# A two-layer decoder step on one core: scores of two heads side by side, running sums as split products, samples' values by transposes

## The chip, the cores and the metric

The kernel runs on one core of a Trainium2 chip. The metric is the device time of one execution in microseconds, as the median of several executions. TensorE multiplies (PE in the profile; its weight loads are PEld), VectorE (DVE), ScalarE (ACT) and GpSimd (POOL) do the rest, and SyncE (SP) issues most transfers.

## What is computed

Two layers of a decoder for a prompt of 256 tokens and eight samples of one token each (position 256), which share all weights: 264 columns in all. Layer 0 mixes by softmax attention in blocks (with 256 keys there is one block, so it is plain causal attention) beside a gated MLP over positions; layer 1 by stick-breaking attention beside causal pooling. After each comes a feed-forward block with a short convolution. Cut to the two attentions:

```
# layer 0, per head
s = q @ k.T * scale;  s = where(causal, s, -inf);  out = softmax(s) @ v
# layer 1, per head
z = q @ k.T * scale
log_keep = where(before, log_sigmoid(-z), 0)
later    = reverse_cumsum(log_keep) - log_keep
w        = where(before, exp(log_sigmoid(z) + later), 0);  out = w @ v
```

A sample's query attends to 256 cached keys, which lie in two pages of 128 per sample, and in layer 0 to its own key as well.

## The kernel before, in words

Activations lie with the features on the 128 partitions and the 264 columns along the free dimension. Every projection is a sum over blocks of 128 x 128 weights. Each weight and each activation is split into a rounded fp32r part and the fp32r rest (h and l), and each block takes three products of 264 columns, h·h, h·l and l·h (lines 334 to 336, the tile mm). The weights come by DMA in chunks; ScalarE makes wh (L311) and VectorE wl (L312) for eight blocks at a time, up to three such tiles ahead, in four buffers.

The order of the projections is fixed by `run`: it goes through the blocks of a phase, and after every eighth block (with fractions allowed) it calls the hooks entered for that point. A hook's number is the count of groups of eight blocks done, less one. The phases are in0, out0, ff0, dn0, in1, out1, ff1, dn1. The hooks hold everything else: page loads, scores, softmax, products with V, the mixers. They only give the order in which the program is written; a planner then places the instructions of each engine by a simulation of its own, as operands and buffers become free, and may move a hook's work behind later projection blocks. Instructions wrapped in `keep_in_program_order` keep their order among each other. Each engine then runs its list strictly in the planned order. PSUM has eight banks: four for projections (psm), four for all else (psa, made by `at`).

What the change touches:

- `s_qk` (lines 650 to 667), layer 0, one head: scores of query block 0 with key block 0 (L654, 128 columns) and of query block 1 with both key blocks (L655, 256 columns), fp32 with 64 rows of contraction, then two bf16 products of the identity with the causal mask (L656, L657), all in one bank; then two maxima on VectorE, two exponentials with sums on ScalarE, and the scaling, into a tile p. `s_tr` transposes p on TensorE (L675), `s_av` multiplies with V (L499, L500).
- `z_qk` (864 to 874), layer 1, one head: scores with keys on the partitions (L868, 256 columns; L869, 128), the masks (L870, L871), and `softplus` (858 to 862: three ScalarE steps, one VectorE step) into L.
- `z_cum` (876 to 882): the reverse running sum along the keys, as a product of a triangle of -1 with L (L880, 384 columns, fp32) and of all -1 with the second key block (L881, 128 columns, fp32), added onto the scores in their bank, and one exponential (L882) into w. Hooks: z_qk of head h at 5 + h, z_cum one hook later.
- The samples: `sample_score` (L456) in column groups of 32, `sample_av` (L470) the products with V, of which VectorE keeps each head's own 64 columns by a mask (L472), and `sample_out` (L483), which gathers them by products with a selection matrix of 8 columns. `sm_out` (721) and `zs_out` (913) put the result into the columns 256 to 263 of catA. In layer 0 sample scores come at hooks 6.5 and 9, their softmax at 10.25; in layer 1 `zs_soft` and `zs_cum` come at 11 and 12, the products with V at 13 and 14.

catA and catB are the operands of the output projection, which reads catB first.

Of the kernel before, what the change touches and what calls it, by code (L numbers as in the profile page):

```python
# [9 lines left out]
F32 = mybir.dt.float32  # L10
F32R = mybir.dt.float32r
# [7 lines left out]
P = 128  # L19
# [3 lines left out]
NS = 8  # L23
# [20 lines left out]
YD = ((0, 1), (1, 2), (2, 4), (4, 6), (6, 8))  # L44
YQ = 1

SC0 = 6.5
SC1 = 9
SGL = 6
GG = 16  # L50
GM = 12
# [1 line left out]
GN = 16.1  # L53
SQK = 5
STR = 7
SSO = 10.25
STP = 12
GT = 17
GA = 17.5
# [11 lines left out]
ZQ1 = 1  # L71
ZC = 1
PM = 13
ZSS = 11
ZSC = 12
ZSA = 13
ZSO = 14.75
NA = 4
# [95 lines left out]
def _consts():  # L174
    f = np.float32
    parts = []

    def add(name, a):
        full = np.zeros((P, a.shape[1]), f)
        full[: a.shape[0]] = a  # L180
        _CST[name] = (sum(x.shape[1] for x in parts), a.shape[1])
        parts.append(full)

    half = 8
    inv = (f(500000.0) ** (-(np.arange(half, dtype=f) * f(2.0) / f(16)))).astype(f)
# [15 lines left out]
    add("bm", (r[:, None] % 32 == h8[None, :]).astype(f))  # L201
    add("selS", np.concatenate([(r[:, None] // 32 + 4 * g == h8[None, :]) for g in range(2)], 1).astype(f))
# [24 lines left out]
def tile_decoder_step(ctx: ExitStack, tc: tile.TileContext, a):  # L227
# [4 lines left out]
    rawp = ctx.enter_context(tc.tile_pool(name="rawp", bufs=3))  # L232
    wsp = ctx.enter_context(tc.tile_pool(name="wsp", bufs=4))
    up = ctx.enter_context(tc.tile_pool(name="up", bufs=24))
    pp = ctx.enter_context(tc.tile_pool(name="pp", bufs=6))
    sm = ctx.enter_context(tc.tile_pool(name="sm", bufs=3))
    psm = ctx.enter_context(tc.tile_pool(name="psm", bufs=MMB, space=PSUM))
    psa = ctx.enter_context(tc.tile_pool(name="psa", bufs=8 - MMB, space=PSUM))
# [226 lines left out]
    def sample_av(msk, pz, vtiles, gr, name):  # L465
        pv = at(f"pv_{name}{gr}")
        for pg in range(NPG):
            for j in range(4):
                sq = 4 * gr + j
                pe.matmul(pv[32 * j:32 * j + 32, :], pz[:, pg, sq, :], vtiles[sq][:, pg, :],  # L470
                          start=pg == 0, stop=pg == NPG - 1)
        v.tensor_tensor(msk[:, gr], pv.rearrange("p (h d) -> p h d", d=HD),  # L472
                        cst("bm").unsqueeze(2).to_broadcast([P, NH, HD]), ALU.mult)

    def sample_av_of(st, pz, vtiles, gr, name):
        return lambda: sample_av(st["msk"], pz, vtiles, gr, name)

    def sample_out(msk, name):

        po = at(f"po_{name}")  # L480
        for t in range(4):
            for gr in range(2):
                pe.matmul(po[:, t * NS:(t + 1) * NS], msk[:, gr, 2 * t:2 * t + 2, :].rearrange("p h d -> p (h d)"),  # L483
                          cst("selS")[:, gr * NS:(gr + 1) * NS],
                          start=t == 0 and gr == 0, stop=t == 3 and gr == 1, skip_group_check=True)
# [130 lines left out]
    maskb0 = con.tile([P, P], BF16, name="maskb0")  # L616
    maskb1 = con.tile([P, P], BF16, name="maskb1")
    identb = con.tile([P, P], BF16, name="identb")

    def masks():  # L620
        tc.keep_in_program_order(v.tensor_copy(maskb0, cst("m0")))
        v.tensor_copy(maskb1, cst("m1"))
        v.tensor_copy(identb, ident)

    q4, k4, v4 = f4("q4"), f4("k4"), f4("v4")
# [21 lines left out]
    vt = f4("vt0", (P, 2, 512))  # L647
    catA, catB = mv("catA0"), mv("catB0")

    def s_qk(h):  # L650
        t, b = h // 2, 64 * (h % 2)
        qh, kh = q4[b:b + 64, t, :], k4[b:b + 64, t, :]
        ps = at(f"S0_{h}")
        pe.matmul(ps[:, 0:P], qh[:, 0:P], kh[:, 0:P], start=True, stop=False, skip_group_check=True)  # L654
        pe.matmul(ps[:, P:384], qh[:, P:SEQ], kh[:, 0:SEQ], start=False, stop=False, skip_group_check=True)  # L655
        pe.matmul(ps[:, 0:P], identb, maskb0, start=False, stop=False, skip_group_check=True)  # L656
        pe.matmul(ps[:, SEQ:384], identb, maskb0, start=False, stop=True, skip_group_check=True)  # L657
# [49 lines left out]
    def sm_tr():  # L707
# [11 lines left out]
        st0["msk"] = f4("msk0", (P, 2, NH, HD))  # L719

    def sm_out():
        po = sample_out(st0["msk"], "l0")
# [67 lines left out]
    def sm_q():  # L790
        st0["qz"] = sample_q(q4, "l0")

    def sm_score(i):
        if i == 0:
            st0["sc"] = at("sc0")
        sample_score(st0["sc"], st0["qz"], ktiles, range(4 * i, 4 * i + 4))

    hk.at(SQ, sm_q)
    hk.at(SC0, sm_score, 0)
    hk.at(SC1, sm_score, 1)  # L800
    hk.at(SGL, sgu_load)
    hk.at(MSK, masks)
    hk.at(GG, gm_gelu)
    hk.at(GM, gm_mean)
    hk.at(GV, gm_var)
    hk.at(GN, gm_norm)
    for h in range(NH):
        hk.at(SQK + h // 2, s_qk, h)
        hk.at(STR + h // 2, s_tr, h)
    hk.at(SSO, sm_soft)  # L810
    hk.at(STP, sm_tr)
# [43 lines left out]
    icnt = cst("icnt").rearrange("p (g i) -> p g i", g=4)  # L855
    st1 = {}

    def softplus(e, z):
        s.activation(e, z, AF.Abs)
        s.activation(e, e, AF.Exp, scale=-1.0)  # L860
        s.activation(e, e, AF.Ln, bias=1.0)
        v.scalar_tensor_tensor(e, z, 0.0, e, ALU.max, ALU.add)

    def z_qk(h):
        t, b = h // 2, 64 * (h % 2)
        qh, kh = q4[b:b + 64, t, :], k4[b:b + 64, t, :]
        ps = at(f"Z1_{h}")
        pe.matmul(ps[:, 0:SEQ], kh[:, 0:P], qh[:, 0:SEQ], start=True, stop=False, skip_group_check=True)  # L868
        pe.matmul(ps[:, SEQ:384], kh[:, P:SEQ], qh[:, P:SEQ], start=False, stop=False, skip_group_check=True)  # L869
        pe.matmul(ps[:, 0:P], identb, maskb1, start=False, stop=False, skip_group_check=True)  # L870
        pe.matmul(ps[:, SEQ:384], identb, maskb1, start=False, stop=False, skip_group_check=True)  # L871
        L = pp.tile([P, 384], F32, tag="p", name=f"L1_{h}")
        softplus(L, ps[:, :384])
        st1["z", h] = (ps, L)

    def z_cum(h):
        ps, L = st1.pop(("z", h))
        if h % 2 == 0:
            st1["w", h // 2] = f4(f"w1_{h // 2}", (P, 2, 384))
        pe.matmul(ps[:, 0:384], cst("negU"), L, start=False, stop=False, skip_group_check=True)  # L880
        pe.matmul(ps[:, P:SEQ], nones, L[:, SEQ:384], start=False, stop=True, skip_group_check=True)  # L881
        s.activation(st1["w", h // 2][:, h % 2, :], ps[:, :384], AF.Exp)  # L882

    def z_av(t):
# [21 lines left out]
    def zs_cum():  # L906
# [4 lines left out]
        st1["msk"] = f4("msk1", (P, 2, NH, HD))  # L911

    def zs_out():
        po = sample_out(st1["msk"], "l1")
# [50 lines left out]
    for n in range(8):  # L965
        hk.at(VL1 + n, drip_of(vload, 2))
    hk.at(SQ1, zs_score)
    for h in range(NH):
        hk.at(ZQ0 + ZQ1 * h, z_qk, h)
        hk.at(ZQ0 + ZQ1 * h + ZC, z_cum, h)  # L970
    hk.at(8, lambda: nc.sync.dma_start(a["k1"], k4))
    for t in range(4):
        hk.at(PM - t, pool_mix, t)
# [94 lines left out]
```

## Time and profile before

| what | us |
|---|---|
| median of 3 runs (lowest, highest) | 633.56 (632.65, 635.03) |
| the profiled execution | 632.96 |
| its span in the profile | 630.9 |
| mean granted TensorE clock in it | 0.994 |
| VectorE busy, ScalarE busy | 413.2, 343.8 |

The profile gives one execution. In the lines that follow later, a timeline row has the start and the length in us, the engine, the line of the kernel, the operation, output<-input by the program's names, the shapes and the count of instructions merged into the row. The recorded length of a product holds its way through the array, so it is longer than the time until the next one may start; start to start is what it costs. fp32 products appear as two instructions, fp32r and bf16 products as one.

### The profile page before, as it was taken

How to read it: one execution, taken by the hardware profiler on the slowest of the kernel's cores; microseconds unless marked ns; L12 is line 12 of the kernel's file. 1: busy time of each engine (PE TensorE's matmuls, PEld its weight loads, DVE VectorE, ACT ScalarE, POOL GpSimd, SP SyncE). 2: the span in 40 equal slices, each digit the busy share in tenths (PEclk: the TensorE clock that was granted, in tenths of full speed). 3: DMA queues.
4: the chain of work that ended last, by engine and by line, in shares of the span. 5: the costliest groups of instructions: out<-in, count | busy, mean ns of one | idle time of the engine just before them, and what ended most of it. 6: DMA issues, size and time to landing. Idle time of an engine off the chain costs nothing.

```text
span 630.9 us, 12406 instructions
## 1 busy us (share of the span) xinstructions
PE 611.6 (97%) x4956; PEld 583.2 (92%) x4956; DVE 413.2 (65%) x690; ACT 343.8 (54%) x608; POOL 82.5 (13%) x111
## 2 busy tenths in 40 slices
PE   7899999998999999999999999999899999999994
PEld 5887997998999999999998886999899999999994
DVE  6895674959966676655654674396996667664442
ACT  6448653667665555644442664366766555564441
POOL 3320132324000000010110000032400000001021
PEclk8999999999999999999999999999999999999998
DMA  7995673543555455795477679354355545554501
GB/s 271 324 414 223 238 262 72 182 156 132 200 201 180 161 195 198 228 382 202 179 189 300 230 117 112 129 172 169 128 200 200 179 166 191 201 165 177 200 1 70
DMA packets 40971, 121.42 MB, mean 192 GB/s; under 512 B 17490, under 2 KB 18642, under 8 KB 29522
## 3 DMA queue, kind: packets, MB, share of 16 engines
q1 hardware_dynamic: 40050, 119.15, 57.2%
q10 hardware_dynamic: 864, 1.49, 0.7%
q8 instruction: 39, 0.64, 0.4%
q14 instruction: 18, 0.15, 0.1%
HBM read 116.68 MB, written 3.94 MB: 191 GB/s over the span
## 4 chain that ended last, share of the span: by engine, by line
PE 90%; DVE 4%; ACT 2%; DMA 2%; issue 1%; POOL 1%; SPq 0%; DVEq 0%; ACTq 0%; POOLq 0%
PE mm L334 27%; PE mm L335 27%; PE mm L336 26%; DMA raw<-in_w 2%; DVE wl L312 1%; PE pv_l L470 1%; PE sc L456 1%; ACT wh L311 1%; PE Z L880 1%; PE Z L868 1%; PE pav L499 1%; DVE xn_l L379 1%; PE S L655 1%; PE S L654 1%; PE po_l L483 1%
## 5 line engine op out<-in xcount | busy, mean ns | idle before, releaser
L312 DVE TENSOR_TENSOR wl<-raw,wh 128x1024 fp32r<-128x1024 f32 x183 | 229.1, 1253 | 135.1 <-ACT wh L311 135.1
L311 ACT ACTIVATE wh<-raw 128x1024 fp32r<-128x1024 f32 x183 | 193.4, 1059 | 204.9 <-PE mm L335 187.6
L335 PE MATMUL mm<-xn_l,wh 128*128 128x264 f32 x544 | 154.4, 284 | 0.0
L336 PE MATMUL mm<-xn_h,wl 128*128 128x264 f32 x544 | 154.1, 283 | 0.0
L334 PE MATMUL mm<-xn_h,wh 128*128 128x264 f32 x544 | 153.9, 283 | 0.0
L334 PEld LDWEIGHTS mm<-xn_h,wh 128*128 128x128 f32 x544 | 102.3, 188 | 0.0
L335 PEld LDWEIGHTS mm<-xn_l,wh 128*128 128x128 f32 x544 | 102.3, 188 | 0.0
L336 PEld LDWEIGHTS mm<-xn_h,wl 128*128 128x128 f32 x544 | 102.2, 188 | 0.0
L335 PE MATMUL mm<-a_l,wh 128*128 128x264 f32 x352 | 99.9, 284 | 0.0
L336 PE MATMUL mm<-a_h,wl 128*128 128x264 f32 x352 | 99.7, 283 | 0.0
L334 PE MATMUL mm<-a_h,wh 128*128 128x264 f32 x352 | 99.5, 284 | 0.0
L335 PEld LDWEIGHTS mm<-a_l,wh 128*128 128x128 f32 x352 | 66.2, 188 | 0.0
L336 PEld LDWEIGHTS mm<-a_h,wl 128*128 128x128 f32 x352 | 66.2, 188 | 0.0
L334 PEld LDWEIGHTS mm<-a_h,wh 128*128 128x128 f32 x352 | 66.1, 188 | 0.0
L334 PE MATMUL mm<-xg_h,wh 128*128 128x264 f32 x160 | 46.9, 300 | 4.2 <-ACT wh L311 2.5
L334 PE MATMUL mm<-xg_f_h,wh 128*128 128x264 f32 x160 | 46.2, 289 | 4.5 <-DVE wk L558 4.3
L335 PE MATMUL mm<-xg_l,wh 128*128 128x264 f32 x160 | 45.6, 291 | 0.0
L336 PE MATMUL mm<-xg_f_h,wl 128*128 128x264 f32 x160 | 45.3, 283 | 0.0
L335 PE MATMUL mm<-xg_f_l,wh 128*128 128x264 f32 x160 | 45.3, 283 | 0.0
L336 PE MATMUL mm<-xg_h,wl 128*128 128x264 f32 x160 | 45.2, 294 | 0.1
L334 PE MATMUL mm<-xg_n_h,wh 128*128 128x264 f32 x128 | 37.9, 296 | 0.0
L335 PE MATMUL mm<-xg_n_l,wh 128*128 128x264 f32 x128 | 37.0, 289 | 0.0
(257 smaller groups left out, 1088.5 us busy)
## 6 DMA issues: line engine op xcount, KB each, us to landing
raw<-in_w SPq DMA_DIRECT2D x89, 1024.0 KB, 4.8
K<-in_kt SPq DMA_DIRECT2D x32, 256.0 KB, 6.2
V<-in_vp SPq DMA_DIRECT2D x32, 256.0 KB, 5.4
raw<-in_w SPq DMA_DIRECT2D x5, 512.0 KB, 5.1
CST<-in_cst SPq DMA_DIRECT2D x1, 560.0 KB, 4.7
XG<-in_x ACTq DMA_DIRECT2D x1, 528.0 KB, 7.7
out_k<-k SPq DMA_DIRECT2D x1, 528.0 KB, 8.7
out_v<-v SPq DMA_DIRECT2D x1, 528.0 KB, 3.0
```

Of the source, the lines that this page charges most:

```text
L311: s.activation(h, src, AF.Copy)
L312: v.tensor_tensor(l, src, h.bitcast(F32), ALU.subtract)
L334: pe.matmul(o, h[:, c:c + P], xh, start=first, stop=False)
L335: pe.matmul(o, h[:, c:c + P], xl, start=False, stop=False)
L336: pe.matmul(o, l[:, c:c + P], xh, start=False, stop=left[m] == 0)
L379: j = v.scalar_tensor_tensor(l, src, gain, h.bitcast(F32), ALU.mult, ALU.subtract)
L456: pe.matmul(ps[32 * t:32 * t + 32, :PAST].rearrange("p (g k) -> p g k", g=NPG), qz[:, t, sq, :], kt[sq][:, :, t * P:(t + 1) * P], start=sq ...
L470: pe.matmul(pv[32 * j:32 * j + 32, :], pz[:, pg, sq, :], vtiles[sq][:, pg, :], start=pg == 0, stop=pg == NPG - 1)
L483: pe.matmul(po[:, t * NS:(t + 1) * NS], msk[:, gr, 2 * t:2 * t + 2, :].rearrange("p h d -> p (h d)"), cst("selS")[:, gr * NS:(gr + 1) * NS ...
L499: pe.matmul(o, vt[:, 0, h * HD:(h + 1) * HD], w[:, :SEQ], start=True, stop=False)
L654: pe.matmul(ps[:, 0:P], qh[:, 0:P], kh[:, 0:P], start=True, stop=False, skip_group_check=True)
L655: pe.matmul(ps[:, P:384], qh[:, P:SEQ], kh[:, 0:SEQ], start=False, stop=False, skip_group_check=True)
```

## The change

Three edits, and what goes with them.

1. Scores by pairs. `s_qk` and `z_qk` now take a tile t, that is two heads, whose q and k lie on partitions 0 to 63 and 64 to 127. Each head has a bank. The mask comes first, as one bf16 product of 384 columns per head that opens the bank (the mask tiles are widened to 384 columns, zeros in the middle), then the two heads' products of one shape one behind the other, then those of the other shape. The four score products keep their program order. The softmax part becomes `s_soft`.
2. Running sums as split products. `z_cum` splits L into lh and ll, both fp32r (ScalarE copies, VectorE subtracts), and multiplies the triangle and the ones, now fp32r constants, with each: four fp32r products for two fp32 ones.
3. Samples' values by transposes. `sample_av` copies the whole product on ScalarE, with no mask. `sample_out` makes four transposes per group of four samples into one bank, 126 columns apart, so that the wanted entries of all heads lie 32 columns apart; four small operations then take them out, half a tile and one group each.

Hooks: sample scores of layer 0 all at 9, their softmax at 9.5; zs_soft at 4.75, zs_cum at 6. z_qk of tile t at 5 + 2t, z_cum of its heads one and two hooks later. The pool of p and L tiles has four buffers instead of six, and two each for lh and ll.

```diff
-SC0 = 6.5
-SC1 = 9
+SC0 = 9
-SSO = 10.25
+SSO = 9.5
-ZSS = 11
-ZSC = 12
+ZSS = 4.75
+ZSC = 6
...
-    pp = ctx.enter_context(tc.tile_pool(name="pp", bufs=6))
+    pp = ctx.enter_context(tc.tile_pool(name="pp", bufs=4))
...
-        v.tensor_tensor(msk[:, gr], pv.rearrange("p (h d) -> p h d", d=HD),
-                        cst("bm").unsqueeze(2).to_broadcast([P, NH, HD]), ALU.mult)
+        s.activation(msk[:, gr], pv, AF.Copy)
...
-        po = at(f"po_{name}")
-        for t in range(4):
-            for gr in range(2):
-                pe.matmul(po[:, t * NS:(t + 1) * NS], msk[:, gr, 2 * t:2 * t + 2, :].rearrange("p h d -> p (h d)"),
-                          cst("selS")[:, gr * NS:(gr + 1) * NS],
-                          start=t == 0 and gr == 0, stop=t == 3 and gr == 1, skip_group_check=True)
-        return po[:, :4 * NS].rearrange("p (t s) -> p t s", s=NS)
+        out = []
+        for gr in range(2):
+            po = at(f"po_{name}{gr}")
+            for t in range(4):
+                pe.transpose(po[:, 126 * t:126 * t + P], msk[:, gr, t * P:(t + 1) * P], ident)
+            for c in range(2):
+                out.append((64 * c, 4 * gr, po[64 * c:64 * c + 64, c::32].rearrange("p (t s) -> p t s", s=4)))
+        return out
...
+    def heads(t):
+
+        return [(q4[b:b + 64, t, :], k4[b:b + 64, t, :]) for b in (0, 64)]
+
+    def s_qk(t):
+        pss, hd = [at(f"S0_{2 * t + i}") for i in range(2)], heads(t)
+        for ps in pss:
+            pe.matmul(ps[:, :384], identb, maskb0, start=True, stop=False, skip_group_check=True)
+        for ps, (qh, kh) in zip(pss, hd):
+            tc.keep_in_program_order(pe.matmul(ps[:, 0:P], qh[:, 0:P], kh[:, 0:P], start=False, stop=False, skip_group_check=True))
+        for ps, (qh, kh) in zip(pss, hd):
+            tc.keep_in_program_order(pe.matmul(ps[:, P:384], qh[:, P:SEQ], kh[:, 0:SEQ], start=False, stop=True, skip_group_check=True))
+        for i, ps in enumerate(pss):
+            s_soft(2 * t + i, ps)
...
-        v.tensor_tensor(osam, osam, po, ALU.add)
+        for b, q, po in sample_out(st0["msk"], "l0"):
+            o = osam[b:b + 64, :, q:q + 4]
+            v.tensor_tensor(o, o, po, ALU.add)
...
+    negU = con.tile([P, P], F32R, name="negU")
+    v.tensor_copy(negU, cst("negU"))
+    nonesr = con.tile([P, P], F32R, name="nonesr")
+    v.tensor_copy(nonesr, nones)
...
+        for ps in pss:
+            pe.matmul(ps[:, :384], identb, maskb1, start=True, stop=False, skip_group_check=True)
+        for ps, (qh, kh) in zip(pss, hd):
+            tc.keep_in_program_order(pe.matmul(ps[:, 0:SEQ], kh[:, 0:P], qh[:, 0:SEQ], start=False, stop=False, skip_group_check=True))
+        for ps, (qh, kh) in zip(pss, hd):
+            tc.keep_in_program_order(pe.matmul(ps[:, SEQ:384], kh[:, P:SEQ], qh[:, P:SEQ], start=False, stop=False, skip_group_check=True))
...
-        pe.matmul(ps[:, 0:384], cst("negU"), L, start=False, stop=False, skip_group_check=True)
-        pe.matmul(ps[:, P:SEQ], nones, L[:, SEQ:384], start=False, stop=True, skip_group_check=True)
+        lh = pp.tile([P, 384], F32R, tag="ph", name=f"Lh_{h}", bufs=2)
+        ll = pp.tile([P, 384], F32R, tag="pl", name=f"Ll_{h}", bufs=2)
+        halves(lh, ll, L)
+        for x in (lh, ll):
+            pe.matmul(ps[:, 0:384], negU, x, start=False, stop=False, skip_group_check=True)
+            pe.matmul(ps[:, P:SEQ], nonesr, x[:, SEQ:384], start=False, stop=x is ll, skip_group_check=True)
...
-        s.activation(osam, po, AF.Copy)
+        for b, q, po in sample_out(st1["msk"], "l1"):
+            v.tensor_copy(osam[b:b + 64, :, q:q + 4], po)
```

More of the change, by code (lines that the diff above doesn't have):

```diff
@@ L614, in tile_decoder_step @@
     v.tensor_tensor(rope[:, 1, :], CS[:, 1, :], R, ALU.mult)
-    maskb0 = con.tile([P, P], BF16, name="maskb0")
-    maskb1 = con.tile([P, P], BF16, name="maskb1")
+    maskb0 = con.tile([P, 384], BF16, name="maskb0")
+    maskb1 = con.tile([P, 384], BF16, name="maskb1")
     identb = con.tile([P, P], BF16, name="identb")
     def masks():
-        tc.keep_in_program_order(v.tensor_copy(maskb0, cst("m0")))
-        v.tensor_copy(maskb1, cst("m1"))
+        tc.keep_in_program_order(v.tensor_copy(maskb0[:, 0:P], cst("m0")))
+        v.tensor_copy(maskb0[:, SEQ:384], cst("m0"))
+        v.tensor_copy(maskb1[:, 0:P], cst("m1"))
+        v.tensor_copy(maskb1[:, SEQ:384], cst("m1"))
+        for mk in (maskb0, maskb1):
+            g.memset(mk[:, P:SEQ], 0.0)
         v.tensor_copy(identb, ident)
@@ L648, in tile_decoder_step, with s_soft @@
     catA, catB = mv("catA0"), mv("catB0")
[L650 to L657, printed above, removed]
+    def heads(t):
[10 more added lines that the diff above has]
+            s_soft(2 * t + i, ps)
+    def s_soft(h, ps):
         st = sm.tile([P, 4], F32, tag="st", name=f"st0_{h}")
@@ L718, in sm_tr @@
         st0["ob"] = ob
-        st0["msk"] = f4("msk0", (P, 2, NH, HD))
+        st0["msk"] = f4("msk0", (P, 2, 512))
     def sm_out():
-        po = sample_out(st0["msk"], "l0")
         osam = sm.tile([P, 4, NS], F32, tag="osam", name="osam", bufs=1)
         v.tensor_tensor(osam, st0["ob"], v4[:, :, SEQ:T], ALU.mult)
-        v.tensor_tensor(osam, osam, po, ALU.add)
+        for b, q, po in sample_out(st0["msk"], "l0"):
+            o = osam[b:b + 64, :, q:q + 4]
+            v.tensor_tensor(o, o, po, ALU.add)
         halves(catA[0][:, :, SEQ:T], catA[1][:, :, SEQ:T], osam)
@@ L791, in sm_q, with sm_score @@
         st0["qz"] = sample_q(q4, "l0")
[L793 to L796, printed above, removed]
+    def sm_score():
+        st0["sc"] = at("sc0")
+        sample_score(st0["sc"], st0["qz"], ktiles, range(NS))
     hk.at(SQ, sm_q)
-    hk.at(SC0, sm_score, 0)
-    hk.at(SC1, sm_score, 1)
+    hk.at(SC0, sm_score)
     hk.at(SGL, sgu_load)
@@ L806, in tile_decoder_step @@
     hk.at(GN, gm_norm)
+    for t in range(4):
+        hk.at(SQK + t, s_qk, t)
     for h in range(NH):
-        hk.at(SQK + h // 2, s_qk, h)
         hk.at(STR + h // 2, s_tr, h)
@@ L862, in softplus, with z_qk @@
         v.scalar_tensor_tensor(e, z, 0.0, e, ALU.max, ALU.add)
[L864 to L874, printed above, removed]
+    def z_qk(t):
+        pss = [at(f"Z1_{2 * t + i}") for i in range(2)]
+        hd = [(q4[b:b + 64, t, :], k4[b:b + 64, t, :]) for b in (0, 64)]
+        for ps in pss:
[4 more added lines that the diff above has]
+            tc.keep_in_program_order(pe.matmul(ps[:, SEQ:384], kh[:, P:SEQ], qh[:, P:SEQ], start=False, stop=False, skip_group_check=True))
+        for i, ps in enumerate(pss):
+            L = pp.tile([P, 384], F32, tag="p", name=f"L1_{2 * t + i}")
+            softplus(L, ps[:, :384])
+            st1["z", 2 * t + i] = (ps, L)
     def z_cum(h):
@@ L910, in zs_cum @@
         to_pz(pc, AF.Exp)
-        st1["msk"] = f4("msk1", (P, 2, NH, HD))
+        st1["msk"] = f4("msk1", (P, 2, 512))
     def zs_out():
-        po = sample_out(st1["msk"], "l1")
         osam = sm.tile([P, 4, NS], F32, tag="osam", name="osam1", bufs=1)
-        s.activation(osam, po, AF.Copy)
+        for b, q, po in sample_out(st1["msk"], "l1"):
+            v.tensor_copy(osam[b:b + 64, :, q:q + 4], po)
         halves(catA[0][:, :, SEQ:T], catA[1][:, :, SEQ:T], osam)
@@ L967, in tile_decoder_step @@
     hk.at(SQ1, zs_score)
-    for h in range(NH):
-        hk.at(ZQ0 + ZQ1 * h, z_qk, h)
-        hk.at(ZQ0 + ZQ1 * h + ZC, z_cum, h)
+    for t in range(4):
+        hk.at(ZQ0 + 2 * ZQ1 * t, z_qk, t)
+        for h in (2 * t, 2 * t + 1):
+            hk.at(ZQ0 + ZQ1 * h + ZC, z_cum, h)
     hk.at(8, lambda: nc.sync.dma_start(a["k1"], k4))
```

2 lines of the change are left out of this document (removed).

## The prediction

> **What bounds the kernel now.** I read the page first, then who waited on TensorE, then the chain and TensorE's timeline around each edit, then the busy time by stage.
>
> ```profile
> span 630.9 us, 12406 instructions
> PE 611.6 (97%) x4956; PEld 583.2 (92%) x4956; DVE 413.2 (65%) x690; ACT 343.8 (54%) x608; POOL 82.5 (13%) x111
> PE 90%; DVE 4%; ACT 2%; DMA 2%; issue 1%; POOL 1%; SPq 0%; DVEq 0%; ACTq 0%; POOLq 0%
> ```
> TensorE is busy for 97% of the span, and 90% of the chain that ended last is its own work. A busy PE in these records need not be a full one, so the list of its waits comes next:
>
> ```profile
> PE mm L334 <- DVE wk L558: 4.3, 4, 1.6
> PE mm L334 <- ACT wh L311: 2.5, 1, 2.5
> PE mm L334 <- DVE q L636: 1.7, 1, 1.7
> ```
> These are the three longest (total, times, longest), and none of them is at a score, a running sum or a sample product: L558 is in the FFN, L311 splits weights, L636 takes a q tile out of PSUM. Around the change TensorE goes from one instruction to the next. So I price every edit in TensorE time, from start to start, and subtract it from the end; what the other engines do is free as long as TensorE is not made to wait. The profiled execution took 632.96 us (span 630.9, and 2.0 around it); the median of the three timed runs is 633.56, 0.6 above it. About 0.5% (3.2 us) is what a measurement of this kernel can tell from no change.
>
> **Layer 0 scores (s_qk).** Four heads stand in a row here:
>
> ```profile
> 36.97 0.28 PE L334 MATMUL mm<-xg_h,wh 128*128 128x264 f32 x1
> 37.18 0.48 PE L654 MATMUL S<-k,q 64*128 64x128 f32 x2
> 37.51 0.59 PE L655 MATMUL S<-k,q 64*128 64x256 f32 x2
> 38.03 0.23 PE L656 MATMUL S<-maskb,identb 128*128 128x128 bf16 x1
> ...
> 41.53 0.28 PE L336 MATMUL mm<-xg_h,wl 128*128 128x264 f32 x1
> 41.66 0.29 PE L334 MATMUL mm<-xg_h,wh 128*128 128x264 f32 x1
> ```
> A projection product steps by 0.12 us (41.53 to 41.66). From 36.97 to 41.53 are 4.56 us, of which two such steps (the one before the scores and the one just after) are not the scores': 4.32 for four heads, 1.08 each, 8.6 for eight. One head: 0.33 for the 128 columns, 0.52 for the 256 (0.43 of streaming and some 0.09 for leaving the 64-row form), the rest masks. Entering the 64-row form costs another 0.09 (36.97 to 37.18 less 0.12).
>
> After: per pair two masks of 384 bf16 columns, then head 0 and head 1 on rows 0-63 and 64-127 in two banks. No row has a 384-column bf16 product; between 0.12 x 384/264 = 0.17 (a one-pass product like mm) and 0.32 (one pass of the 384-column product below) I take 0.17, since mm too goes through in one pass. If the two heads run beside each other, a pair costs what one head cost: 0.34 + 0.09 + 0.33 + 0.52 = 1.28 in place of 2.16. Saved: 4 x 0.88 = 3.5.
>
> Whether they do is the main unknown, as no row has two row groups at once (the masks over all 128 rows stand between heads). The bounds are both at once, and one after the other: two more passes of 0.11 and two of 0.215, 1.93 a pair. The nearest rows are those with column groups:
>
> ```profile
> 341.65 3.66 PE L456 MATMUL sc<-K,qz_l 128*32 128x256 f32 x64
> 345.24 0.48 PE L868 MATMUL Z<-q4b,k4b 64*128 64x256 f32 x1
> ...
> 391.89 0.66 PE L499 MATMUL pav<-w,vt 128*64 128x256 f32 x4
> 392.37 0.40 PE L500 MATMUL pav<-w,vt 128*64 128x128 f32 x4
> ```
> 64 passes of 256 columns on four column groups take 3.59, 0.056 each instead of 0.215: 3.8 of 4 go on at once. Four passes on two column groups start the next line after 0.48, where 0.86 would be serial. I take full overlap by these. The Trainium skill (TensorE: Matmul & The Clock Gate, Part 3) gives 3.07x for four row tiles of 32 rows; no run here shows row tiles yet.
>
> **Layer 1 scores (z_qk).**
>
> ```profile
> 346.87 0.28 PE L336 MATMUL mm<-xg_n_h,wl 128*128 128x264 f32 x1
> 347.08 0.70 PE L868 MATMUL Z<-q4b,k4b 64*128 64x256 f32 x2
> 347.62 0.38 PE L869 MATMUL Z<-q4b,k4b 64*128 64x128 f32 x2
> 347.93 0.23 PE L870 MATMUL Z<-maskb,identb 128*128 128x128 bf16 x1
> ...
> 348.24 0.28 PE L335 MATMUL mm<-xg_n_l,wh 128*128 128x264 f32 x1
> ```
> A head that stands alone costs 1.37 - 0.24 = 1.13. A pair after: 0.34 + 0.09 + 0.54 + 0.31 = 1.28. Saved: 4 x (2.26 - 1.28) = 3.9; without overlap 1.93 a pair, 1.3 saved.
>
> **Running sums (z_cum).**
>
> ```profile
> 353.24 0.28 PE L334 MATMUL mm<-xg_n_h,wh 128*128 128x264 f32 x1
> 353.37 0.81 PE L880 MATMUL Z<-L,CST 128*128 128x384 f32 x2
> 354.01 0.38 PE L881 MATMUL Z<-L,nones 128*128 128x128 f32 x2
> ...
> 354.35 0.29 PE L336 MATMUL mm<-xg_n_h,wl 128*128 128x264 f32 x1
> ```
> A head costs 1.11 - 0.24 = 0.87: fp32 goes in two passes. After, lh and ll are one fp32r pass each: 0.17 for 384 columns by mm's rate, and for 128 columns a time that no row has: between 0.055 (mm's rate) and 0.22 (both fp32 passes of L881). I take 0.11, one fp32 pass at the same shape. 2 x 0.28 = 0.56, saved 0.31 x 8 = 2.5; with 0.22 only 0.7. Added beside it: per head one ScalarE copy (lh) and one VectorE subtraction (ll), weighed below.
>
> **Samples' values (sample_out).**
>
> ```profile
> 103.32 1.85 PE L483 MATMUL po_l<-CST,msk 128*128 128x8 f32 x16
> 105.03 0.37 PE L334 MATMUL mm<-catB_h,wh 128*128 128x264 f32 x1
> ...
> 59.11 0.28 PE L336 MATMUL mm<-xg_h,wl 128*128 128x264 f32 x1
> 59.24 0.49 PE L675 MATMUL pt<-CST,p 128*128 128x128 f32 x3
> ...
> 59.69 0.29 PE L335 MATMUL mm<-xg_l,wh 128*128 128x264 f32 x1
> ```
> Sixteen passes of 8 columns take 1.71, 0.107 each: the weights' load, not the 8 columns. Three transposes cost 0.58 - 0.24 = 0.34, 0.11 each. Eight transposes instead: 0.9, saved 0.8 a layer, 1.6 in all. The Trainium skill (the same page, Part 4) has about 275 ns for a transpose in a kernel; sixteen at that would be 4.4, a loss of 1.0. By it the whole sum below would be 8.4 and the time 625.2; the rows contradict it as a cost (0.11 from start to start), so I give it no chance.
>
> ```profile
> 94.56 3.64 PE L470 MATMUL pv_l<-V,PZ 128*32 128x512 f32 x32
> ...
> 108.54 0.28 PE L334 MATMUL mm<-catA_h,wh 128*128 128x264 f32 x1
> ```
> The mask product leaves VectorE, and ScalarE gets a copy instead; four small adds (layer 0) or copies (layer 1) replace one operation. In layer 0 their result is wanted by the first catA product, at 108.54, 3.5 us behind the end of po_l, and TensorE has catB products until then, so I cost them at nothing; without that cover it would be about 0.5 once.
>
> **What only moves.** The samples' scores are joined at hook 9, and zs_soft and zs_cum come six hooks earlier: the same products on TensorE, with projection products on both sides, so nothing. K0 tiles are held longer, and SP's V0 loads that take their buffers start later, but V is first read at 94.56. With four p buffers in place of six, the third pair's exponentials wait for the first pair's transposes (L675); projections fill TensorE meanwhile, and if they didn't, a pair would lose the length of a head's softmax once. The wider masks and the two fp32r constants are four more small copies on VectorE and two memsets on POOL, off the path. The pinned score products may draw a projection product between two of them; each such split costs about 0.18 (out of the 64-row form and in again), and I allow 0.5 in all for three.
>
> **Sum:** 3.5 + 3.9 + 2.5 + 1.6 - 0.5 = 11.0. The profiled execution would become 622.0, the median 633.56 - 11.0 = **622.6**.
>
> **Rivals.**
>
> *Half overlap.* If the two passes of one head are issued before those of the other, and products start in order, only the second pass of head 0 lies beside the first of head 1. By the rows that is one 256-column pass (0.215) more a pair: 1.5. Saved: 4 x 0.66 + 4 x 0.76 + 2.5 + 1.6 - 0.5 = 9.3, **624.3**. The Trainium skill (TensorE: Matmul & The Clock Gate, Part 3) says that matmuls keep program order, and that only weight loads are pulled ahead. Against it: the four L499 passes would then take 0.64, and took 0.48. Chance 0.2.
>
> *No overlap: the change doesn't do what it says.* Saved 4 x 0.23 + 1.3 + 2.5 + 1.6 - 0.5 = 5.8, **627.8**. For it: no row with row groups. Chance 0.14.
>
> *VectorE becomes the bound* while layer 1's pool sums run:
>
> ```profile
> 360.00:370.00 10.00, 10.00 (x71) 8.77 (x70) 8.77 (x28) 6.98 (x13) 0.53 (x5) 1.00 0.78 278
> ACT wh L311 <- PE mm L335: 28.9, 21, 4.6
> L860 ACT ACTIVATE L<-L x8: 515/526/535, 346.9 to 381.3; 128x384 f32<-128x384 f32 x8
> L862 DVE SCALAR_TENSOR_TENSOR L<-Z,L x8: 548/554/559, 349.6 to 382.5; 128x384 f32<-128x384 f32 x8
> ```
> In these 10 us (columns: PE, PEld, DVE, ACT, POOL) VectorE has 8.77 of work. Two subtractions of some 0.55 (L862's shape) make 9.9, and TensorE needs 1.6 less (a pair and two sums), 8.4: short by 1.5, about 3.0 over the two such stretches, and **625.6** if nothing covers it. Against it: the split of the weights waited for TensorE to free a buffer all 21 times from 326 to 431 us, so it runs up to three tiles (3 x 8 blocks x 0.36 = 8.7 us) ahead. Chance 0.08.
>
> *Slower: the running sums come too early in TensorE's order.* Place: z_cum in layer 1. TensorE takes its instructions in order, so if the sums stand one hook (2.9 us) behind their scores and ll isn't there, everything behind them waits, the projections and the bank release included. From a pair's scores to the second ll: six ScalarE steps of 0.5 (L860), one VectorE 0.55, the copy 0.5, the subtraction 0.55, so 4.7, and with two weight splits of 1.06 ahead on ScalarE 6.8. That is 3.9 a pair, 15.6 in all: 633.56 - 11.0 + 15.6 = **638.2**; it is a loss from 2.75 a pair. Two banks are held by each pair meanwhile, of four. Against it:
>
> ```profile
> 364.70 0.56 DVE L862 SCALAR_TENSOR_TENSOR L<-Z,L 128x384 f32<-128x384 f32 x1
> ...
> 368.51 0.81 PE L880 MATMUL Z<-L,CST 128*128 128x384 f32 x2
> ```
> L is ready at 365.26 and used at 368.51: the planner leaves 3 us and fills them with projections. Chance 0.08.
>
> **How the numbers follow.** Forecast 0.50 (622.6, within 9.3 and 12), half overlap 0.2, none 0.14, VectorE 0.08, slower 0.08. The slow end of the 128-column fp32r pass (1.8) can join any of them. Faster by over 0.5%: all but the last, less 0.05 for two rivals at once, 0.87; within 0.5%: 0.06; slower: 0.07. The range must leave out no more than 0.2: from 620.5 (a 128-column pass at 0.055 and no split pairs) to 628.5 (no overlap, and something over).
>
> **What would show it.** Pairs: the next product 1.3 us after a pair's masks begin, and the two heads' first passes starting within 0.02 us; 0.2 apart means half, and a pair of 1.9 none. Sums: 0.56 a head; 0.78 if the short pass is slow. Eight transposes in 0.9. Any wait of TensorE for ll, lh or a score's bank in layer 1 would speak for the last rival; VectorE at 10 of 10 with TensorE waiting for wl, for the third. The prediction is wrong altogether if TensorE's waits grow by over 7 us.

## The result and the profile after

| | before | after |
|---|---|---|
| median, us (lowest to highest) | 633.54 (632.65 to 635.03) | 623.25 (622.63 to 623.85) |
| span of the profiled execution, us | 630.9 | 621.0 |
| mean granted TensorE clock in it | 0.994 | 0.995 |

The ratio is 0.9833, with a 95% interval from 0.9814 to 0.9853: 10.3 us faster, where 11.0 were forecast (622.6; range 620.5 to 628.5). Line numbers from here on are those of the changed kernel: the projection is L331 to L333, the masks of the scores L658 and L882, the scores L660/L662 (layer 0) and L884/L886 (layer 1), the running sums L900/L901, the transposes of the samples' values L480.

The head of the page after:

```profile
span 621.0 us, 12353 instructions
PE 599.9 (97%) x4924; PEld 575.6 (93%) x4924; DVE 412.3 (66%) x705; ACT 349.6 (56%) x621; POOL 83.0 (13%) x113
```

TensorE lost 11.7 us of busy time and stayed at 97%: it was the bound and still is. VectorE's time is the same within 1 us, ScalarE has 5.8 more, and neither shows in the end. The waits of TensorE (total, times, longest):

```profile
PE mm L331 <- DVE wk L555: 4.3, 4, 1.6
...
PE S L658 <- ACT p L672: 0.3, 1, 0.3
```

The first is an old one. The only new wait at a changed place is 0.3 us of a mask for its bank, until the exponential that reads an earlier head's scores there and writes p (L672) is done. No wait for lh or ll is on the list.

**Layer 0.** TensorE's timeline where the first two pairs stand together, and the passes of L660 that start between 38.15 and 38.17 (count, shortest/median/longest in ns, first and last start):

```profile
37.94 0.28 PE L331 MATMUL mm<-xg_h,wh 128*128 128x264 f32 x1
38.16 0.49 PE L660 MATMUL S<-k,q 64*128 64x128 f32 x4
38.48 0.60 PE L662 MATMUL S<-k,q 64*128 64x256 f32 x4
38.91 0.39 PE L660 MATMUL S<-k,q 64*128 64x128 f32 x4
39.14 0.60 PE L662 MATMUL S<-k,q 64*128 64x256 f32 x4
39.67 0.39 PE L332 MATMUL mm<-xg_l,wh 128*128 128x264 f32 x1
39.89 0.29 PE L333 MATMUL mm<-xg_h,wl 128*128 128x264 f32 x1
```
```profile
L660 PE MATMUL S<-k,q x2: 373/373/373, 38.2 to 38.2; 64*128 64x128 f32 x2
```

From 37.94 to 39.89 are 1.95; less two projection steps of 0.12, four heads' scores cost 1.71. Four passes of 256 columns (two heads of two passes each) take 0.43, from 38.48 to 38.91: before, one head's two passes took that. Two passes start within 0.02 us, the two heads' first ones (their records have 7 ns between them).

**Layer 1.** The first pair, and the third, which is cut:

```profile
345.00 0.49 PE L882 MATMUL Z<-maskb,identb 128*128 128x384 bf16 x2
345.42 0.70 PE L884 MATMUL Z<-q4b,k4b 64*128 64x256 f32 x4
345.95 0.39 PE L886 MATMUL Z<-q4b,k4b 64*128 64x128 f32 x4
346.27 0.39 PE L333 MATMUL mm<-xg_n_h,wl 128*128 128x264 f32 x1
346.50 0.28 PE L331 MATMUL mm<-xg_n_h,wh 128*128 128x264 f32 x1
...
360.80 0.70 PE L884 MATMUL Z<-q4b,k4b 64*128 64x256 f32 x2
361.43 0.45 PE L900 MATMUL Z<-Lh,negU 128*128 128x384 f32 x1
...
361.86 0.70 PE L884 MATMUL Z<-q4b,k4b 64*128 64x256 f32 x2
362.49 0.44 PE L900 MATMUL Z<-Lh,negU 128*128 128x384 f32 x1
...
362.92 0.49 PE L886 MATMUL Z<-q4b,k4b 64*128 64x128 f32 x4
```

The first pair takes 346.50 - 345.00 - 0.12 = 1.38. In the third, the running sums of two earlier heads stand between head 0's 256 columns, head 1's, and the rest: each group of two passes is alone again (0.63 until the next line) and the 64-row form is left and entered twice more.

**Sums and transposes.**

```profile
354.94 0.28 PE L331 MATMUL mm<-xg_n_h,wh 128*128 128x264 f32 x1
355.06 0.34 PE L900 MATMUL Z<-Lh,negU 128*128 128x384 f32 x1
355.24 0.22 PE L901 MATMUL Z<-Lh,nonesr 128*128 128x128 f32 x1
355.30 0.33 PE L332 MATMUL mm<-xg_n_l,wh 128*128 128x264 f32 x1
355.47 0.28 PE L333 MATMUL mm<-xg_n_h,wl 128*128 128x264 f32 x1
...
390.96 0.66 PE L480 MATMUL po_l<-CST,msk 128*128 128x128 f32 x4
391.38 0.37 PE L332 MATMUL mm<-catB_l,wh 128*128 128x264 f32 x1
```

Half a running sum costs 355.47 - 354.94 - 0.24 = 0.29, so 0.58 a head in place of 0.87, and the 128-column fp32r pass is not slow. The first four transposes of layer 1 step on in 0.42. Not every half sum is that cheap: those that stand behind other small products, and not between projection products, cost more. Here the last two heads' halves follow one another:

```profile
382.44 0.45 PE L900 MATMUL Z<-Ll,negU 128*128 128x384 f32 x1
...
382.90 0.44 PE L900 MATMUL Z<-Lh,negU 128*128 128x384 f32 x1
```

This half takes 0.46 until the next one. The four halves of the last two heads cost 1.81 by their own steps, where four between projection products cost 4 x 0.24 = 0.96.

**Where the time went.** Two stages hold everything that the change touches: from the start of the 40th projection block's third product to that of the 224th (most of in0, and out0), and from the 752nd to the 944th (in1 and out1). After, these products are the following; before, they start at 27.39, 125.89, 321.30 and 425.86.

```profile
28.42 0.29 PE L333 MATMUL mm<-xg_h,wl 128*128 128x264 f32 x1
...
122.56 0.28 PE L333 MATMUL mm<-catA_h,wl 128*128 128x264 f32 x1
...
317.78 0.29 PE L333 MATMUL mm<-a_h,wl 128*128 128x264 f32 x1
...
416.34 0.28 PE L333 MATMUL mm<-catA_h,wl 128*128 128x264 f32 x1
```

So 98.50 became 94.14 in layer 0 and 104.56 became 98.56 in layer 1: -4.4 and -6.0. Between and behind them 0.6 more was won, and 1.0 was lost ahead of the first of these four products, in the part of the kernel that begins with the first transfers; its start lay between 26.9 and 28.4 in all kernels here, edits or none. Together -9.9, the difference of the spans. Each instruction's time to the next start, summed by what it writes, says what the two stages are made of (us):

| | layer 0 before | after | layer 1 before | after | layer 1, samples late (below) |
|---|---|---|---|---|---|
| scores | 6.81 | 3.22 | 6.79 | 4.23 | 3.41 |
| masks | 1.27 | 1.00 | 0.83 | 1.34 | 1.47 |
| running sums | | | 6.96 | 5.13 | 4.09 |
| samples' values gathered (po) | 1.71 | 0.79 | 1.62 | 0.85 | 0.85 |
| samples' products with V (pv) | 3.57 | 3.57 | 4.68 | 3.71 | 3.71 |
| projection | 70.18 | 70.62 | 73.35 | 72.89 | 72.89 |

What isn't listed moved by less than 0.2 in sum in each layer. The time that TensorE needs to get out of the 64-row form falls in two places: 0.1 on the last score product (0.53 from 39.14 to 39.67, where the same row took 0.43 from 38.48 to 38.91) and 0.1 on the projection product behind it (0.22 at 39.67 and 0.23 at 346.27, where a step is 0.12). The second part stands under projection in the table.

### The profile page after: what moved, and what is told of

The parts are those of the page before. It is cut to its first block, busy times and chain, and to the rows that moved or that the text cites. A ratio compares the mean times of both kernels' runs of the same rounds, so it can differ in the third digit from the quotient of the medians.

```text
span 621.0 us, 12353 instructions
## 1 busy us (share of the span) xinstructions
PE 599.9 (97%) x4924; PEld 575.6 (93%) x4924; DVE 412.3 (66%) x705; ACT 349.6 (56%) x621; POOL 83.0 (13%) x113
## 4 chain that ended last, share of the span: by engine, by line
PE 86%; DVE 5%; issue 2%; DMA 2%; ACT 2%; POOL 1%; SPq 0%; DVEq 0%; ACTq 0%
PE mm L331 27%; PE mm L332 26%; PE mm L333 26%; DVE wl L309 2%; DMA XG<-in_x 1%; PE pv_l L467 1%; PE sc L453 1%; DMA raw<-in_w 1%; ACT wh L308 1%; PE pav L496 1%; PE Z L900 1%; DVE xn_l L376 1%; PE Z L884 1%; POOL wk L554 0%; PE pt L684 0%
## 5 line engine op out<-in xcount | busy, mean ns | idle before, releaser
L331 PE MATMUL mm<-xn_h,wh 128*128 128x264 f32 x544 | 153.9, 284 | 0.0
L333 PE MATMUL mm<-xn_h,wl 128*128 128x264 f32 x544 | 153.8, 283 | 0.0
L333 PEld LDWEIGHTS mm<-xn_h,wl 128*128 128x128 f32 x544 | 102.4, 188 | 0.0
L331 PEld LDWEIGHTS mm<-xn_h,wh 128*128 128x128 f32 x544 | 102.1, 188 | 0.0
L331 PE MATMUL mm<-a_h,wh 128*128 128x264 f32 x352 | 99.6, 284 | 0.0
L333 PE MATMUL mm<-a_h,wl 128*128 128x264 f32 x352 | 99.6, 283 | 0.0
L333 PEld LDWEIGHTS mm<-a_h,wl 128*128 128x128 f32 x352 | 66.2, 188 | 0.0
L331 PEld LDWEIGHTS mm<-a_h,wh 128*128 128x128 f32 x352 | 66.1, 188 | 0.0
L331 PE MATMUL mm<-xg_h,wh 128*128 128x264 f32 x160 | 46.6, 298 | 4.5 <-ACT wh L308 2.0
L331 PE MATMUL mm<-xg_f_h,wh 128*128 128x264 f32 x160 | 46.3, 289 | 4.5 <-DVE wk L555 4.3
L333 PE MATMUL mm<-xg_h,wl 128*128 128x264 f32 x160 | 44.7, 291 | 1.1 <-DVE wl L309 1.1
L333 PE MATMUL mm<-xg_f_h,wl 128*128 128x264 f32 x160 | 45.3, 283 | 0.0
L331 PE MATMUL mm<-xg_n_h,wh 128*128 128x264 f32 x128 | 37.4, 292 | 0.0
L333 PE MATMUL mm<-xg_n_h,wl 128*128 128x264 f32 x128 | 36.8, 288 | 0.0
```

Source lines behind the costliest of these rows:

```text
L331: pe.matmul(o, h[:, c:c + P], xh, start=first, stop=False)
L333: pe.matmul(o, l[:, c:c + P], xh, start=False, stop=left[m] == 0)
```

## The experiments

Ratios are to the kernel before on the same chip.

**Edit 1 alone** (scores by pairs; hooks, sums and samples as before):

```diff
-    for h in range(NH):
-        hk.at(SQK + h // 2, s_qk, h)
+    for t in range(4):
+        hk.at(SQK + t, s_qk, t)
```

> The kernel before with edit 1 alone (scores by pairs, mask first; hooks and sums as before). My theory, TensorE time saved by two heads running beside each other: 8 pairs at 1.28 us in place of 2.16 (layer 0) and 2.26 (layer 1), 3.5 + 3.9 = 7.4 us less, so about 626.1. Rival, the gain is only that the masks are joined and the 64-row form is entered once a pair: 1.93 a pair, 2.2 us less, about 631.3.

Measured: 627.95, ratio 0.9924 (0.9912 to 0.9937), 5.0 saved. Layer 1 (752nd to 944th block) gave 3.7, where 3.9 was expected, but not by the scores alone: scores and masks gave 2.6 and the projection products around them 0.9, together 3.5; pv gave 1.0 as in the next run, and 0.8 was lost in the products of w with V. The scores of layer 0 cost 3.22, exactly as in the changed kernel, but in0 gave only 1.0. The timeline shows why:

```profile
41.65 1.93 PE L456 MATMUL sc<-K,qz_l 128*32 128x256 f32 x32 [1.10 <-POOL rz_k L643]
```

The samples' scores, still at hook 6.5, now stand close behind the shorter scores, and TensorE meets them 1.1 us before POOL has their operand. The other half of them is cut by masks and transposes into groups of 10, 8 and 14; all sample scores of layer 0 together cost 4.73 in place of 4.04. So the edit brings the gain and the hooks are needed to keep it, if that is the cause; the run "edit 1 with the hooks" below tests it.

**Edit 2 alone** (running sums as split products):

```diff
-        pe.matmul(ps[:, 0:384], cst("negU"), L, start=False, stop=False, skip_group_check=True)
-        pe.matmul(ps[:, P:SEQ], nones, L[:, SEQ:384], start=False, stop=True, skip_group_check=True)
+        halves(lh, ll, L)
+        for x in (lh, ll):
+            pe.matmul(ps[:, 0:384], negU, x, start=False, stop=False, skip_group_check=True)
+            pe.matmul(ps[:, P:SEQ], nonesr, x[:, SEQ:384], start=False, stop=x is ll, skip_group_check=True)
```

> The kernel before with edit 2 alone (running sums as split fp32r products, and the smaller p pool). My theory: 8 x (0.87 - 0.56) = 2.5 us less, about 631.0, with no wait of TensorE for lh or ll. Rival, the added copy and subtraction make TensorE wait or bind VectorE beside the pool sums: no gain or a loss, 633.5 or more.

Measured: 630.52, ratio 0.9965 (0.9953 to 0.9978). In the trace in1 and out1 are 3.7 shorter: the running sums went from 6.96 to 3.84 while the projection products behind them took 0.65 more, net 2.5, and pv went from 4.68 to 3.71. No term had the second. By time the run gained 2.4, where 2.5 was expected, and that closeness is in part luck: 0.2 was lost ahead of the two stages and 0.9 behind them, in projection blocks that no edit touches (23.41 in place of 23.20 for 64 blocks, from the 1072nd to the 1264th). Before, one head's sum stood inside the 16 products of pv:

```profile
384.79 1.91 PE L470 MATMUL pv_l<-V,PZ 128*32 128x512 f32 x10
386.63 0.91 PE L880 MATMUL Z<-L,CST 128*128 128x384 f32 x2
387.38 0.39 PE L881 MATMUL Z<-L,nones 128*128 128x128 f32 x2
387.69 1.06 PE L470 MATMUL pv_l<-V,PZ 128*32 128x512 f32 x6
```

With edit 2 they stand together:

```profile
386.86 1.92 PE L470 MATMUL pv_l<-V,PZ 128*32 128x512 f32 x16
388.71 0.39 PE L334 MATMUL mm<-xg_n_h,wh 128*128 128x264 f32 x1
```

Sixteen take 1.85. In two pieces, ten took 1.84 and six 0.99 (387.69 to the projection at 388.68), 2.83 without the sum: products that go side by side on four column groups lose 1.0 to a full-width guest.

**Edit 3 alone** (samples' values by transposes):

```diff
-        v.tensor_tensor(msk[:, gr], pv.rearrange("p (h d) -> p h d", d=HD),
-                        cst("bm").unsqueeze(2).to_broadcast([P, NH, HD]), ALU.mult)
+        s.activation(msk[:, gr], pv, AF.Copy)
...
+                pe.transpose(po[:, 126 * t:126 * t + P], msk[:, gr, t * P:(t + 1) * P], ident)
```

> The kernel before with edit 3 alone (no mask on VectorE, eight transposes a layer instead of sixteen narrow passes). My theory: 2 x (1.71 - 0.9) = 1.6 us less, about 631.9. Rival, the four small operations that take the values out come late for the output projection: no gain, 633.5.

Measured: 631.78, ratio 0.9989 (0.9976 to 1.0001). By time alone this is not told from nothing. In the trace out0 became 0.87 shorter and in1 with out1 0.87: 1.7, as priced.

**The hooks alone** (the kernel before with the change's hooks of the samples):

```diff
-SC0 = 6.5
+SC0 = 9
...
-SSO = 10.25
+SSO = 9.5
...
-ZSS = 11
-ZSC = 12
+ZSS = 4.75
+ZSC = 6
```

> The kernel before with only the hooks moved (all sample scores of layer 0 at 9, their softmax at 9.5, layer 1 samples' softmax at 4.75 and 6). My theory: the same TensorE work in another place, no difference, 633.5 within 0.5. Rival, the earlier samples relieve the end of in1: 1 us or more less.

Measured: 632.73, ratio 0.9999 (0.9986 to 1.0011). By themselves the moves are worth nothing.

**Edit 1 with the hooks:**

> The kernel before with edit 1 (scores by pairs) and the moved hooks of the samples (sample scores of layer 0 at 9, their softmax at 9.5, zs_soft at 4.75, zs_cum at 6), without edits 2 and 3. Theory: the hooks alone are worth nothing (ratio 0.9999), but edit 1 needs them: with the sample scores left at 6.5, the pairs alone gave only 1.0 of the 3.5 in layer 0, because TensorE met the sample scores behind the faster pairs and waited. Then 633.0 - 3.5 - 3.9 = 625.6. Rival: the loss in layer 0 of the pairs alone had another cause, and 628 stays.

Measured: 625.71, ratio 0.9895 (0.9876 to 0.9913), where 625.6 was expected. in0 is 3.55 shorter, in1 with out1 3.77. The wait for rz_k is gone. So the moved hooks of layer 0's samples are part of edit 1's gain: nothing alone, 2.5 of in0 with it. That the time meets the expectation so well is in part luck: of layer 1's 3.77, 1.0 is pv again, and one pair of layer 1 is cut here as well (its scores cost 4.03 in all, against 3.41 in the run with edit 1 alone).

**The order of a pair's products, head after head.** The loops of L660/L662 and of L884/L886 become one, so that all of head 0's products stand ahead of head 1's:

```diff
         for ps, (qh, kh) in zip(pss, hd):
             tc.keep_in_program_order(pe.matmul(ps[:, 0:P], qh[:, 0:P], kh[:, 0:P], start=False, stop=False, skip_group_check=True))
-        for ps, (qh, kh) in zip(pss, hd):
             tc.keep_in_program_order(pe.matmul(ps[:, P:384], qh[:, P:SEQ], kh[:, 0:SEQ], start=False, stop=True, skip_group_check=True))
```

> The changed kernel, with one difference: in a pair, both products of head 0 come before both of head 1 (same products, same masks, same banks). My theory, the gain of edit 1 is overlap of row groups: only the middle two products can lie beside each other, so a pair costs 0.43 us more for the two layers' intact pairs, 3 us (626.2), up to 0.65 a pair or 5 us (628) if nothing overlaps. Rival, joined masks and fewer changes of form make the gain: no difference, 623.2.

Measured: 622.09, ratio 0.9832 (0.9819 to 0.9845): no slower than the change. The expectation fell. The timeline, and the passes of L660 (its 128-column line) that start between 37.14 and 37.17:

```profile
36.94 0.28 PE L331 MATMUL mm<-xg_h,wh 128*128 128x264 f32 x1
37.15 0.50 PE L660 MATMUL S<-k,q 64*128 64x128 f32 x4
37.47 0.61 PE L661 MATMUL S<-k,q 64*128 64x256 f32 x4
37.91 0.49 PE L660 MATMUL S<-k,q 64*128 64x128 f32 x4
38.13 0.70 PE L661 MATMUL S<-k,q 64*128 64x256 f32 x4
38.76 0.39 PE L332 MATMUL mm<-xg_l,wh 128*128 128x264 f32 x1
```
```profile
L660 PE MATMUL S<-k,q x2: 373/373/373, 37.1 to 37.2; 64*128 64x128 f32 x2
```

Two 128-column passes start together, though in the kernel's order both passes of one head's 256-column product stand between the two heads' 128-column ones. In the second pair the first passes start together too, and from the second pass on one head runs some 0.11 behind the other and still beside it. From 36.94 to 38.76 are 1.82, in the changed kernel 1.73. The Trainium skill (TensorE: Matmul & The Clock Gate, Part 3) has products in strict order, none overtaking another; by that rule, if the chip were given the kernel's order, the first pair would have half its overlap, and this trace shows it whole. Whether TensorE takes the two row groups from its queue apart, or the order is changed on the way to the chip, no view here tells.

**Scores not pinned** (the four products of a pair keep no order among each other, so the planner places them):

```diff
-            tc.keep_in_program_order(pe.matmul(ps[:, 0:P], qh[:, 0:P], kh[:, 0:P], start=False, stop=False, skip_group_check=True))
+            pe.matmul(ps[:, 0:P], qh[:, 0:P], kh[:, 0:P], start=False, stop=False, skip_group_check=True)
```

> The changed kernel without keep_in_program_order on the score products. The planner then sets mask and both products of one head ahead of the other head's in five of the eight pairs. My theory: overlap is lost there, 5 x 0.65 = 3.3 us, less one pair that the pinned plan had split itself: about 626. If pinning doesn't matter on the chip: 623.2.

Measured: 628.91, ratio 0.9941 (0.9925 to 0.9957). It lost 5.7 against the change, more than half its gain. The planner put the second head's mask between the heads in five of eight pairs, and such a head is alone:

```profile
44.41 0.34 PE L658 MATMUL S<-maskb,identb 128*128 128x384 bf16 x1
44.68 0.49 PE L660 MATMUL S<-k,q 64*128 64x128 f32 x2
45.01 0.59 PE L662 MATMUL S<-k,q 64*128 64x256 f32 x2
```
```profile
PE S L658 <- ACT p L672: 1.2, 1, 1.2
```

The counts are 2 and 2 where the change has 4 and 4. The scores of layer 0 cost 4.91 in place of 3.22, and a mask waits 1.2 for its bank. In the two stages the trace is 5.3 longer than the change: 3.4 of it are the scores (in layer 1 5.94 in place of 4.23), near the 3.3 expected; masks took 1.1 more, the projection 1.3, and pv, in two pieces again, 1.0, and 1.0 came back in the running sums. So it is the overlap that saves, and a full-row product between the two heads takes it away.

**One more split per head.** The change with the split of L into lh and ll done twice (the same values again), to see how much room ScalarE and VectorE still have:

```diff
         halves(lh, ll, L)
+        halves(lh, ll, L)
```

> The changed kernel with the split of L made twice over (the ScalarE copy and the VectorE subtraction repeated into the same tiles), which doubles the work that edit 2 adds to the two engines and makes the path from L to the sums about 1 us longer. My theory: covered by projections, at most 0.5 us more, 623.2 to 623.7, save for pairs that the plan splits or joins otherwise (0.9 each). Rival, VectorE binds beside the pool sums: 8 x 0.55 = 4 us more of its work, 2 to 4 us slower, 625 to 627.

Measured: 624.47, ratio 0.9866 (0.985 to 0.9883), 1.2 over the change, between the two expectations; in1 with out1 are 1.7 longer in the trace. No pair is cut in this plan (the scores of layer 1 cost 3.41, in the change 4.23), so 0.8 was won back beside it, and the second split took some 2.5 of those stages: that lies in the rival's 2 to 4. Busy time (PE, PEld, DVE, ACT, POOL) in its fullest 10 us, then its longest new wait, and last the changed kernel's stretch that answers to the one in the prediction:

```profile
365.00:375.00 10.00, 8.98 (x69) 8.51 (x68) 9.64 (x28) 6.10 (x11) 1.53 (x5) 1.00 0.68 230
```
```profile
PE mm L331 <- ACT catB_h L973: 1.4, 1, 1.4
```
```profile
360.00:370.00 10.00, 10.00 (x71) 8.61 (x70) 7.64 (x23) 6.36 (x13) 0.73 (x5) 1.00 0.55 207
```

One split makes TensorE wait for nothing: VectorE had 7.64 of 10 there in the change, and 9.09 in its fullest stretch, from 375 to 385. A second one does: VectorE is at 9.64 and TensorE waits, though for what ScalarE writes. Ahead of the longest wait ScalarE ran without a break from 380.25 to 382.50, with a split of weights and the doubled copy before catB_h. The added chain went through both engines, so which of the two ran out isn't separated.

**Layer 1's sample sums back at their old hooks,** on the changed kernel:

```diff
-ZSS = 4.75
-ZSC = 6
+ZSS = 11
+ZSC = 12
```

> The changed kernel with the samples' softmax and running sum of layer 1 back at hooks 11 and 12. In the changed kernel's trace the third pair of layer 1 has running sums between its two heads; with this plan all four pairs stand together. My theory: that pair costs about 0.9 less, 622.4, and nothing else changes. Rival, the early place of the samples was worth something by itself: the time rises above 623.2, with waits at the end of the in1 phase.

Measured: 621.2, ratio 0.9818 (0.98 to 0.9837). The plan changes, and all four pairs stand together. It was run again beside the change, with a version that also has the third and fourth pair of layer 0 one hook later:

```diff
-        hk.at(SQK + t, s_qk, t)
+        hk.at(SQK + t + (t > 1), s_qk, t)
```

> The changed kernel unchanged, as the thing to compare with on the same chip: 622.5 to 623.3.

> The changed kernel with zs_soft and zs_cum back at 11 and 12. Theory: the third pair of layer 1 is no longer cut by running sums, the stages in1 and out1 took 2.0 less in the trace, so 1 to 2 below the changed kernel on the same chip, and the two 95% intervals barely overlap. Rival: the first look was one lucky trace, and the two are equal.

> As the run before, and the scores of the third and fourth pair of layer 0 one hook later. Theory: TensorE's wait of 1.0 for the bank of the third pair (mask S, until p of an earlier head has been read) goes, 0.5 to 1.0 less than the run before. Rival: the fourth pair then stands among the samples' scores and the transposes of p, which are cut, and nothing is gained or up to 1 lost.

| | median | ratio (95%) | in0 | in1 and out1 |
|---|---|---|---|---|
| the change again | 622.95 | 0.9851 (0.9836 to 0.9866) | 59.41 | 98.58 |
| samples late | 622.23 | 0.9832 (0.9819 to 0.9846) | 59.31 | 96.60 |
| samples late, pairs late | 621.24 | 0.9813 (0.9799 to 0.9828) | 59.65 | 96.51 |

The third pair with samples late:

```profile
356.59 0.34 PE L882 MATMUL Z<-maskb,identb 128*128 128x384 bf16 x1
356.86 0.70 PE L884 MATMUL Z<-q4b,k4b 64*128 64x256 f32 x4
357.39 0.39 PE L886 MATMUL Z<-q4b,k4b 64*128 64x128 f32 x4
```

In the table of the two stages, scores (3.41 against 4.23) and sums (4.09 against 5.13) give 1.9 of the 2.0 back, and all three traces with late samples have it. Of the 1.0 in the sums only 0.4 is at the cut (two half sums of 0.43 in place of 0.24); 0.6 is at the last two heads, whose four halves cost 1.21 with samples late in place of 1.81. By time, samples late was 0.7 below the change measured beside it, and the first time 2.0 below the change's first measurement; the intervals overlap both times. The version with the later pairs is clear of the change (the intervals don't meet), and is the fastest here; but against samples late alone it shows nothing: in0 is no shorter, and a transpose now waits where the mask waited:

```profile
PE pt L684 <- ACT p L674: 0.9, 1, 0.9
```

## Why the prediction was right, and where it was off

**What bounds it.** Right. TensorE stayed at 97%, and the stages shrank by what its own instructions saved.

**Layer 0 scores, 3.5.** Right: in0 -3.5, and -3.55 with edit 1 and hooks. Full overlap held, as the rows with column groups had it. The Trainium skill (TensorE: Matmul & The Clock Gate, Why this matters for your kernels) has products on different row groups start at most 4 ns apart. The records here have 7 ns in the change and 13 in the first pair of the head-after-head run, which decides for this case; either is small beside a pass of 0.11 us.

**Layer 1 scores, 3.9.** Right in the mechanism for pairs that stand whole, and 0.4 too high: 3.5 in scores, masks and the products around them with edit 1 alone. That the edit as a whole gave 3.7 and 3.8 has pv's 1.0 in it, which the prediction didn't have, and the losses of a new plan. One pair takes 1.38 and not 1.28, since the sum had 0.09 for leaving the 64-row form, and the projection product behind it takes another 0.1.

**Running sums, 2.5.** Right: 2.5 net alone, 0.29 a head less. The 128-column pass, for which no row stood, costs 0.06 and 0.05 on the product behind it, together the 0.11 that was taken.

**Samples' values, 1.6.** Right: 1.7. A transpose costs 0.11 from start to start.

**What only moves, nothing.** True of the hooks alone, false of the hooks together with edit 1: 2.5 us of layer 0's gain hang on the samples' scores having moved.

**Split pairs, -0.5.** The term that was mis-sized. It allowed 0.18 a cut, for the change of form alone. One pair of eight was cut, by two half sums, which would have been 0.36; it cost 1.2: 0.8 in the scores, since the pair loses its overlap too, and 0.4 in the two half sums that stand in between. The same plan cost another 0.6 in the sums of the last two heads, so some 1.9 in all. Of the moved hooks, the early sample sums of layer 1 brought that plan about. The 1.0 of pv, which wasn't forecast, makes up for half of it: 3.5 + 3.5 + 2.5 + 1.7 + 1.0 - 1.9 = 10.3. The mechanism was right in every priced edit; that the total came within 0.7 of the forecast is in part luck, as a term that wasn't there and a term that was too small nearly cancel.

**The rivals.** Half overlap fell with the change's own trace and with the head-after-head order; no overlap fell with the counts of 4. VectorE is not the bound in the change, but it, or ScalarE, is close: one more split costs 1.2 by time, and some 2.5 without the pair that its plan happened to join. Sums too early: TensorE waits for no lh and no ll.

## What to carry to other kernels

When TensorE is the bound and busy all the time, price each edit in its start-to-start time, and then ask of the plan which full-width product may land inside a group that works on part of the array: on 64 rows, or on 32 columns, such a guest costs the group its overlap besides its own time. Pin such groups: without the pins 5.7 of the 10.3 us were lost here, 3.4 of them in the scores themselves. A move that is free by itself can still be what an edit needs, so try an edit with its moves and without.

## What the runs showed of the chip

- Two heads on rows 0 to 63 and 64 to 127, in two banks, cost what one costs: 0.43 for four passes of 64 x 256 fp32. The two heads' products need not stand next to each other in the order of the kernel.
- Getting into the 64-row form costs some 0.1 us (0.22 from 37.94 to 38.16, with a projection step of 0.12), getting out of it some 0.2: 0.1 on the last product in it (0.53 from 39.14 to 39.67 in place of 0.43) and 0.1 on the projection product behind (0.22 from 39.67 to 39.89). The Trainium skill (TensorEngine Tiling (Array Packing), Key Properties) says that a change of the tiling mode drains TensorE; these delays fit that, and no view here shows the drain itself.
- A 128-column fp32r product with new weights steps by 0.06 us (355.24 to 355.30) and delays the next by 0.05 (0.17 from 355.30 to 355.47, with a step of 0.12); one of 384 columns steps by 0.18. No further penalty shows for the short one.
